# A four-layer trunk on one core: keys squared ahead of the tanh, another bank for the bonus product, two value buffers, transposes in pieces, and two copies that change engines

## The chip, the cores and the metric

The kernel runs on one core of a Trainium2 chip. The time is that of one execution on the device, in microseconds (us). Of the kernel before, three runs gave 1247.04, 1248.28 and 1244.97 us, median 1247.04. The traces name the engines PE (TensorE matmul), PEld (its weight loads), DVE (VectorE), ACT (ScalarE), POOL (GpSimd) and SP (SyncE). A name such as `L883` is a line of the kernel; the lines of the changed kernel stand up to two lower.

## The reference, cut to what matters

The trunk has 512 positions of 1024 channels in float32. Its layers are a gated spatial mixer, a gated feed-forward layer with a short convolution, an RWKV-7 time mixer, a second such feed-forward layer, and a last norm. All lines of the change lie in the time mixer:

```python
r = xr @ w_r;  k = xk @ w_k;  v = xv @ w_v
w = -softplus(-(w0 + tanh(xw @ w1) @ w2)) - 0.5      # decay
a = sigmoid(a0 + (xa @ a1) @ a2)
g = sigmoid(xg @ g1) @ g2                            # gate
kk = heads(k * k_k)
kk = kk * rsqrt(maximum(sum(kk * kk, -1), 1e-24))
k = k * (1 + (a - 1) * k_a)
y = wkv7_scan(r, exp(-exp(w)), k, v, -kk, kk * a)    # 16 heads of 64 channels
#   S_t = S_{t-1} diag(w_t) + (S_{t-1} a_t) b_t^T + v_t k_t^T ;  y_t = S_t r_t
y = (y - mean(y)) * rsqrt(var(y) + 64e-5) * ln_w + ln_b
bonus = sum(r_h * k_h * r_k, -1, keepdims=True) * v_h
out = ((y + bonus) * g) @ w_o
```

## The kernel before, in words

Activations lie transposed: 128 channels on the partitions, all 512 positions along the free axis, so that 1024 channels are eight tiles of 128x512. A dense product is made as three matmuls, high part by high part, high by low and low by high (`mm3`, L325, L326 and L327), which keeps float32 accuracy. The four layers run one after another. The accumulator memory (PSUM) is used through four tags, `mm`, `aux`, `e` and `us`, with two banks each; a tile that asks for a bank waits until the tile that held it has been read.

The time mixer replaces the step-by-step recurrence by chunks of 64 positions: within a chunk a triangular system is solved, and a state is handed from chunk to chunk. Its work comes in pieces, written as generators:

- `pairs` goes over the eight pairs of heads p = 0 to 7. For each, `decay` makes the decay factors (tanh, L906, running sum, exponentials) and the norm of the scaled keys (`kn` L908, its square `sq` L913, summed over the head by matmul L923, then L925 and L926). `operands` scales keys and receptances (L944 to L957). `products` makes the triangular blocks (matmul L973, masked on DVE at L977, copied by ACT at L978) and the factors of the state (L986 to L991).
- `projections` makes keys and values with dense matmuls. It is taken a step at a time as a filler between the other pieces. A value's accumulator is copied by ACT (L854) into the tile `v`, and `value` then transposes and centres it (L868, copies L873), multiplies the head sums of r·k (matmul L883) by `v` on DVE (L885) and adds the bias `ln_b` on ACT (L886). The result lies in `rt`, where the gate finds it.
- `invert(g)` inverts the triangular blocks of four pairs (g = 0 or 1). ACT (or DVE) copies the blocks into `ix` (L1046, L1048), DVE transposes them into `li` (L1051), solves 32x32 blocks by a long back-substitution (L1062 to L1070, small operations that depend on one another), and transposes the answer twice (L1051: into `ix` and into `li`). PE then builds the 64x64 inverses (L1090, L1093) with copies on ACT between (L1098, L1103).
- `scan(g)` handles eight chunks: PE L1301, copy `wt` on DVE (L1304), PE L1314 with the inverse, copies L1315 and L1316, PE L1321 and L1327, and so on. `finish` normalises the outputs, and `gate` (L1209) multiplies them by the gate before the output projection.

What order these take is settled when the program is built: the generators are woven, some with a note that they are issued behind a given PE instruction, and a scheduler writes one queue per engine. Each engine then takes its queue in that order. The scheduler's decisions change with every edit, so that an edit on one engine also moves rows on the others.

Of the kernel before, what the change touches and what calls it, by code (L numbers as in the profile page):

```python
# [12 lines left out]
F32 = mybir.dt.float32  # L13
F32R = mybir.dt.float32r
AF = mybir.ActivationFunctionType
ALU = mybir.AluOpType
# [4 lines left out]
P = 128  # L21
D = 1024
KT = 8
T = 512
# [120 lines left out]
class Emit:  # L145
# [622 lines left out]
    def rwkv_main(self, r, ctx, gain):  # L768
# [13 lines left out]
        def tmp(tag, bufs, w=W2):  # L782
            return tile_([P, w], tag, bufs)
# [12 lines left out]
        def second_factors(p):  # L796

            w32 = self.l2w.pop()
            l2[:] = [ep.tile([P, 2 * P], F32R, tag=f"l2{i}", bufs=1, name=self.uid("l2")) for i in range(3)]
            for j in range(2):  # L800
                w = w32[:, 512 * j:512 * j + 2 * P]
                S.copy(l2[j], w)
                V.tensor_tensor(l2[2][H[j]], w[H[j]], l2[j][H[j]].bitcast(F32), ALU.subtract)
            if p + 2 < KT:
                self.load_l2(p + 2)


        def projections():

            load = Ahead([lambda n=n, m=m: self.parts(n, m) for n in PARTS for m in range(KT)])  # L810

            def key(m, a):
                while m >= NKEY and m - NKEY not in used:
                    yield
                ks[m] = tmp("key", NKEY, T)
                S.copy(ks[m], a)

            for m in range(KT - 2):
                a = self.acc("mm")
                yield from self.dense_steps(a, load.take(), r.xk)  # L820
                yield from key(m, a)
                yield

            ws = [load.take(), load.take(False)]
            accs = [self.acc("mm") for _ in range(2)]
            xv = []
            for k in range(KT):
                for j in range(2):
                    self.mm3(accs[j], self.wcols(ws[j], k * P, P), r.xk[k], k == 0, k == KT - 1)
                while len(xv) < min(k + 3, KT):  # L830
                    xv.append(r.mix(3, len(xv)))
                if k == 4:
                    load.fetch()
                yield
            for j in range(2):
                yield from key(KT - 2 + j, accs[j])
            late = iter(())
            for m in range(KT):
                a = self.acc("mm")
                w = load.take()  # L840
                if m == KT - 2:
                    ga["w"] = load_gate(0)
                for n, _ in enumerate(self.dense_steps(a, w, xv)):
                    yield
                    next(late, None)
                    if m == KT - 1 and n == 0:
                        gw[0] = gate_weights(ga["w"])
                        ga["parts"] = self.gate_parts()
                    if m == KT - 1 and len(gx) < 2:
                        gx.append(gate_mix(len(gx)))  # L850
                for _ in late:
                    yield
                v = ip.tile([P, T], F32, tag="v", bufs=1, name=self.uid("v"))
                S.copy(v, a)  # L854
                late = value(m, v)
            next(late)
            tail.append(late)

        def value(m, v):
            g, i = divmod(m, 4)  # L860

            def bank():
                return self.acc("mm" if len(done) < KT else "aux")

            vt = ip.tile([P, NCH, C], F32, tag="vt", bufs=1, name=self.uid("vt"))
            q = bank()
            for b in range(4):
                nc.tensor.matmul(q[:, b * P:(b + 1) * P], v[:, b * P:(b + 1) * P], self.c("center", P),  # L868
                                 start=True, stop=True)
            q4 = q.rearrange("p (b h f) -> p b h f", b=4, h=2)  # L870
            for hd in range(2):
                for par in range(2):
                    S.copy(vt[H[1 - hd], par::2, :], q4[H[par], :, hd, :])  # L873
            nc.sync.dma_start(vtd[:, :, m].rearrange("c p f -> p c f"), vt)
            yield
            yield

            while m not in done:
                yield
            wb = ip.tile([P, P], F32, tag="wb", bufs=1, name=self.uid("wb"))  # L880
            S.activation(wb, self.c("bones", P), AF.Copy, scale=self.p("r_k", m))
            q = bank()
            nc.tensor.matmul(q, wb, rt[g][:, i, :], start=True, stop=True)  # L883
            b = rt[g][:, i, :]
            V.tensor_tensor(b, q, v, ALU.mult)  # L885
            S.activation(b, b, AF.Identity, bias=self.p("ln_b", m))  # L886
            vdone.add(m)
            yield


        def scratch(tag):
            return self.gp.tile([P, T], F32, tag=tag, bufs=2 if tag == "sq" else 1, name=self.uid(tag))

        def decay(p, u):
# [6 lines left out]
                nc.tensor.matmul(accs[j], l2[2][H[j], w], r.lr[j][H[j]], start=False, stop=True)  # L901
            if p % 2 == 1 and p + 1 < KT:
                second_factors(p + 1)
            th, u.ta = scratch("sq"), tmp("ta", 2, T)
            for j, x in enumerate((th, u.ta)):
                S.activation(x, accs[j], AF.Tanh, scale=0.5, bias=dq(j, p))  # L906
            u.kn = tmp("kn", 2, T)
            S.activation(u.kn, k, AF.Copy, scale=dq(2, p))  # L908
            V.tensor_scalar(th, th, 1.0, None, ALU.add)
            yield  # L910
            V.tensor_tensor_scan(th, self.c("smask", T), th, 0.0, ALU.mult, ALU.add)
            sq = scratch("sq")
            S.activation(sq, u.kn, AF.Square)  # L913
            u.gt = tile_([P, NCH, C + 1], "gt", 1)
            G.memset(u.gt[:, :, 0:1], 1.0)
            S.activation(u.gt[:, :, 1:], c3(th), AF.Exp, scale=C1)
# [110 lines left out]
        def invert(g):  # L1027
# [19 lines left out]
                if g == 1 and us.start == 0:  # L1047
                    yield  # L1048
            def turn(out, src):
                for bs in [slice(n, n + 8) for n in range(0, 32, 8)] if g == 1 else [slice(0, 32)]:  # L1050
                    V.transpose(out[:, bs], src[:, bs])  # L1051

            tt = blocks("li")
# [149 lines left out]
        def gate(g, i, ts, q=None):  # L1203

            if q is None:
                q = self.acc("aux")[:, 0:ts.stop - ts.start]
                opening(g, i, ts, q)
            o = rt[g][:, i, ts]
            V.tensor_tensor(o, o, q, ALU.mult)  # L1209
            while len(outs[g]) <= i:  # L1210
                outs[g].append(tuple(self.xr.tile([P, T], F32R, tag=t, bufs=10, name=self.uid(t)) for t in ("mxh", "mxl")))
            oh, ol = (x[:, ts] for x in outs[g][i])
            S.copy(oh, o)
            V.tensor_tensor(ol, o, oh.bitcast(F32), ALU.subtract)
# [52 lines left out]
        def scan(g, late=iter(())):  # L1267
# [15 lines left out]
            for c in range(NCH):  # L1283
# [17 lines left out]
                lead = batch(lambda i, hd, n: nc.tensor.matmul(us[H[hd], 0, i, :], both(i, hd, 0), vu[:, hd, i, :],  # L1301
                                                               start=True, stop=True))
                wt = tile_([P, 4, C], "wt", 4)
                V.tensor_copy(wt, us[:, 0])  # L1304
                batch(lambda i, hd, n: nc.tensor.matmul(e[H[hd], 0, i, :], st[i][H[hd], 0:C], vu[H[hd], hd, i, :],
                                                        start=i == 0, stop=False, skip_group_check=True), lead)
                if not last:
# [217 lines left out]
```

## Time and profile before

| what | us |
|---|---|
| median of three runs | 1247.04 (1244.97 to 1248.28) |
| the profiled execution | 1245.55 |
| its span, first to last instruction | 1243.7 |
| PE busy in the span | 1226.8 (99%) |
| DVE busy | 851.1 (68%) |
| ACT busy | 633.1 (51%) |
| POOL busy | 81.4 (7%) |
| mean granted TensorE clock | 0.996 |

The profile is of one execution; durations are from it. A row of the timeline reads: start in us, duration in us, engine, line, operation, tile written <- tiles read, shape, count, and in brackets the idle time of the engine ahead of it and what ended it. A row of the waits reads: engine, tile and line that waited, engine, tile and line waited for, total us, times, the longest. A row of the windows reads: stretch, its length and busy us (with the number of instructions) of PE, PEld, DVE, ACT and POOL, then the granted clock, the share of the DMA engines' time and GB/s. Matmuls overlap, so that what one costs is read from the distance between two starts. The pairs run from about 572 to 716 us, the first scan from about 725 on, and the time mixer ends near 885.

### The profile page before, as it was taken

How to read it: one execution, taken by the hardware profiler on the slowest of the kernel's cores; microseconds unless marked ns; L12 is line 12 of the kernel's file. 1: busy time of each engine (PE TensorE's matmuls, PEld its weight loads, DVE VectorE, ACT ScalarE, POOL GpSimd, SP SyncE). 2: the span in 40 equal slices, each digit the busy share in tenths (PEclk: the TensorE clock that was granted, in tenths of full speed). 3: DMA queues.
4: the chain of work that ended last, by engine and by line, in shares of the span. 5: the costliest groups of instructions: out<-in, count | busy, mean ns of one | idle time of the engine just before them, and what ended most of it. 6: DMA issues, size and time to landing. Idle time of an engine off the chain costs nothing.

```text
span 1243.7 us, 19411 instructions
## 1 busy us (share of the span) xinstructions
PE 1226.8 (99%) x7535; PEld 1000.2 (80%) x7535; DVE 851.1 (68%) x1418; ACT 633.1 (51%) x1089; POOL 81.4 (7%) x106
## 2 busy tenths in 40 slices
PE   9999999999999999999999999999999999999997
PEld 6878888888888888877887777778888888888886
DVE  5566578888876454675899698776777777872323
ACT  6544455555554343466787667424544444543232
POOL 1100200000000001000000013222000000000000
PEclk9999999999999999999999899999999999999999
DMA  7232457887556776326888797654223223333332
GB/s 273 94 105 82 132 180 246 246 249 241 192 172 193 220 226 196 109 81 182 220 242 237 188 280 233 219 171 135 85 102 102 90 97 102 97 88 104 97 93 81
DMA packets 125133, 201.65 MB, mean 162 GB/s; under 512 B 39857, under 2 KB 63153, under 8 KB 125041
## 3 DMA queue, kind: packets, MB, share of 16 engines
q10 hardware_dynamic: 38976, 112.87, 29.5%
q1 hardware_dynamic: 86064, 87.54, 22.6%
q8 instruction: 59, 0.97, 0.3%
q14 instruction: 34, 0.27, 0.1%
HBM read 152.93 MB, written 47.45 MB: 161 GB/s over the span
## 4 chain that ended last, share of the span: by engine, by line
PE 91%; DVE 4%; DMA 3%; ACT 1%; issue 0%; SPq 0%; POOL 0%; DVEq 0%; POOLq 0%; ACTq 0%
PE mm L325 9%; PE mm L327 9%; PE mm L326 9%; PE aux L325 6%; PE aux L326 6%; PE aux L327 6%; PE e L325 6%; PE e L326 6%; PE us L325 6%; PE e L327 6%; PE us L327 6%; PE us L326 6%; PE us L1314 1%; PE aux L973 1%; PE aux L988 1%; PE us L1321 1%
## 5 line engine op out<-in xcount | busy, mean ns | idle before, releaser
L237 ACT CAST w<-w 128x512 fp32r<-128x512 f32 x340 | 206.5, 611 | 359.8 <-PE aux L327 92.6
L238 DVE TENSOR_TENSOR w<-w,w 128x512 fp32r<-128x512 f32 x340 | 230.5, 680 | 180.2 <-ACT w L237 179.6
L325 PE MATMUL mm<-mxh,w 128*128 128x512 f32 x408 | 167.9, 412 | 2.7 <-DVE rt L885 2.6
L327 PE MATMUL mm<-mxh,w 128*128 128x512 f32 x408 | 161.1, 395 | 0.0
L326 PE MATMUL mm<-mxl,w 128*128 128x512 f32 x408 | 160.6, 394 | 0.0
L325 PEld LDWEIGHTS mm<-mxh,w 128*128 128x128 f32 x408 | 77.0, 189 | 22.8 <-DVE rt L885 3.3
L327 PEld LDWEIGHTS mm<-mxh,w 128*128 128x128 f32 x408 | 77.0, 189 | 17.1 <-issue 0.8
L326 PEld LDWEIGHTS mm<-mxl,w 128*128 128x128 f32 x408 | 77.1, 189 | 16.2 <-issue 1.7
L575 ACT ACTIVATE cv<-z,par 128x512 f32<-128x512 f32 x88 | 71.7, 817 | 26.5 <-DVE z L573 21.2
L325 PE MATMUL aux<-mxh,w 128*128 128x512 f32 x216 | 84.5, 391 | 0.0
L325 PE MATMUL us<-mxh,w 128*128 128x512 f32 x216 | 84.5, 391 | 0.0
L327 PE MATMUL aux<-mxh,w 128*128 128x512 f32 x216 | 84.2, 390 | 0.0
L326 PE MATMUL aux<-mxl,w 128*128 128x512 f32 x216 | 84.1, 389 | 0.0
L326 PE MATMUL us<-mxl,w 128*128 128x512 f32 x216 | 84.1, 389 | 0.0
L327 PE MATMUL us<-mxh,w 128*128 128x512 f32 x216 | 84.1, 389 | 0.0
L354 POOL TENSOR_TENSOR ss<-ss,sq 128x512 f32<-128x512 f32 x24 | 31.7, 1323 | 761.1 <-ACT sq L352 761.1
L325 PE MATMUL e<-mxh,w 128*128 128x512 f32 x208 | 81.4, 391 | 0.0
L326 PE MATMUL e<-mxl,w 128*128 128x512 f32 x208 | 81.1, 390 | 0.0
L327 PE MATMUL e<-mxh,w 128*128 128x512 f32 x208 | 81.0, 389 | 0.0
L576 DVE SCALAR_TENSOR_TENSOR cv<-z,par,cv 128x512 f32<-128x512 f32 x88 | 66.0, 752 | 19.5 <-ACT cv L575 19.5
L577 DVE SCALAR_TENSOR_TENSOR cv<-z,par,cv 128x512 f32<-128x512 f32 x88 | 66.0, 752 | 2.9
L325 PEld LDWEIGHTS aux<-mxh,w 128*128 128x128 f32 x216 | 40.5, 188 | 9.0 <-issue 0.5
(1113 smaller groups left out, 2555.2 us busy)
## 6 DMA issues: line engine op xcount, KB each, us to landing
w<-in_wup ACTq DMA_DIRECT2D x88, 512.0 KB, 3.7
w<-in_wdn ACTq DMA_DIRECT2D x32, 512.0 KB, 3.7
st<-std SPq DMA_DIRECT2D x15, 640.0 KB, 6.6
w<-wkd ACTq DMA_DIRECT2D x16, 512.0 KB, 5.1
w<-wvd ACTq DMA_DIRECT2D x16, 512.0 KB, 5.1
w<-wod ACTq DMA_DIRECT2D x16, 512.0 KB, 4.2
w<-in_wdn ACTq DMA_DIRECT2D x16, 384.0 KB, 3.3
w<-in_wsu ACTq DMA_DIRECT2D x8, 512.0 KB, 3.7
```

The source lines that it names most:

```text
L237: nc.scalar.copy(hi[r, :n], src)
L238: (lo_eng or nc.vector).tensor_tensor(lo[r, :n], src, hi[r, :n].bitcast(F32), ALU.subtract)
L325: mm(acc, wh, xh, start=first, stop=False)
L326: mm(acc, wh, xl, start=False, stop=False)
L327: mm(acc, wl, xh, start=False, stop=last)
L354: nc.gpsimd.tensor_tensor(self.ss, self.ss, self.sq, ALU.add)
L575: nc.scalar.activation(c, z[:, 2:], AF.Identity, scale=cw(2, i), bias=self.p("conv_b", l * 44 + i))
L576: nc.vector.scalar_tensor_tensor(c, z[:, 1:T + 1], cw(1, i), c, ALU.mult, ALU.add)
L577: nc.vector.scalar_tensor_tensor(c, z[:, 0:T], cw(0, i), c, ALU.mult, ALU.add)
L973: nc.tensor.matmul(qs[hd][:, c - ch.start, :], bk[H[hd], c, C * hd:C * hd + P], ar[H[hd], c, :], start=True, stop=True)
L988: nc.tensor.matmul(qs[hd][:, c, :], bk[H[hd], c, C * hd:C * hd + P], dg[H[hd], c, :], start=True, stop=True)
L1314: nc.tensor.matmul((us, ux)[hd][H[hd], 1, i, :], ti[g][H[hd], i, c, :], wt[H[hd], i, :], start=True, stop=True)
```

## The change

It has six parts, all in the time mixer.

1. The value tile `v` gets two buffers.
2. The bank of the bonus product L883 is `aux` when all pairs are done, `e` when the operands of the last pair have been issued, and otherwise `mm`; before, it was `mm` until all pairs were done.
3. The bias `ln_b` is no longer added by ACT in `value`, but inside the gate, whose DVE multiplication becomes a scalar_tensor_tensor (add, then multiply).
4. In `decay`, the scaled key and its square are issued ahead of the two tanh.
5. The transposes of the first inversion are made in four pieces of eight blocks each, as those of the second were.
6. The copy of `wt` in the scan moves from DVE to ACT.

```diff
-                v = ip.tile([P, T], F32, tag="v", bufs=1, name=self.uid("v"))
+                v = ip.tile([P, T], F32, tag="v", bufs=2, name=self.uid("v"))
...
-            q = bank()
+            q = self.acc("aux" if len(done) == KT else "e" if KT - 1 in used else "mm")
             nc.tensor.matmul(q, wb, rt[g][:, i, :], start=True, stop=True)
             b = rt[g][:, i, :]
             V.tensor_tensor(b, q, v, ALU.mult)
-            S.activation(b, b, AF.Identity, bias=self.p("ln_b", m))
...
+            u.kn, sq = tmp("kn", 2, T), scratch("sq")
+            S.activation(u.kn, k, AF.Copy, scale=dq(2, p))
+            S.activation(sq, u.kn, AF.Square)
             th, u.ta = scratch("sq"), tmp("ta", 2, T)
             for j, x in enumerate((th, u.ta)):
                 S.activation(x, accs[j], AF.Tanh, scale=0.5, bias=dq(j, p))
-            u.kn = tmp("kn", 2, T)
-            S.activation(u.kn, k, AF.Copy, scale=dq(2, p))
             V.tensor_scalar(th, th, 1.0, None, ALU.add)
             yield
             V.tensor_tensor_scan(th, self.c("smask", T), th, 0.0, ALU.mult, ALU.add)
-            sq = scratch("sq")
-            S.activation(sq, u.kn, AF.Square)
...
-                for bs in [slice(n, n + 8) for n in range(0, 32, 8)] if g == 1 else [slice(0, 32)]:
+                for bs in [slice(n, n + 8) for n in range(0, 32, 8)]:
                     V.transpose(out[:, bs], src[:, bs])
...
-            V.tensor_tensor(o, o, q, ALU.mult)
+            V.scalar_tensor_tensor(o, o, self.p("ln_b", 4 * g + i), q, ALU.add, ALU.mult)
...
-                V.tensor_copy(wt, us[:, 0])
+                S.copy(wt, us[:, 0])
```

**DVE, where the first inversion begins.** `lq` is the masked block of a pair (pair 5 under the first number, pair 6 under the later one), `sq` its decay argument, `n_963` the norm of pair 6, `li` the transposed blocks. Before:

```order
L977 TENSOR_TENSOR lq_5794<-aux_5784,cst 128x4x128
L977 TENSOR_TENSOR lq_5794<-us_5785,cst 128x4x128
L911 SCALAR_TENSOR_TENSOR sq_5775<-cst,sq_5775 128x512
L1051 STREAM_TRANSPOSE li_5820<-ix_5814 128x32x32
L1055 MEMSET li_5820 128x32
L1062 SCALAR_TENSOR_TENSOR li_5820<-li_5820 128x30
L1069 TENSOR_TENSOR pr_5815<-li_5820 128x58
L925 TENSOR_SCALAR n_963_5837<-e_5832 128x8
```

and in the changed kernel:

```order
L975 TENSOR_TENSOR lq_5796<-us_5787,cst 128x4x128
L909 TENSOR_SCALAR sq_5779<-sq_5779 128x512
L911 SCALAR_TENSOR_TENSOR sq_5779<-cst,sq_5779 128x512
L923 TENSOR_SCALAR n_963_5840<-e_5835 128x8
L924 RECIPROCAL n_963_5840<-n_963_5840 128x8
L975 TENSOR_TENSOR lq_5853<-aux_5843,cst 128x4x128
L1049 STREAM_TRANSPOSE li_5822<-ix_5816 128x8x32 x4
L975 TENSOR_TENSOR lq_5853<-us_5844,cst 128x4x128
L1053 MEMSET li_5822 128x32
```

The norm of pair 6 and the first half of its next mask moved from behind the transposes to in front of them, and the transpose became four. Further down the same queue three of the four pieces of the last transpose (`li_6289<-li_5822`) stand between operations of the back-substitution, where before one whole transpose stood at its end.

**ACT, the same place.** `ix` are the blocks to be inverted, `kn` the scaled key of pair 6 and the `sq` made from it its square, `ta` and the other `sq` the two tanh. Before:

```order
L906 ACTIVATE sq_5775<-e_5769,dpar 128x512
L906 ACTIVATE ta_5776<-e_5770,dpar 128x512
L908 ACTIVATE kn_5779<-key_5738,dpar 128x512
L1046 COPY ix_5814<-ti_4841 32x1024
L957 COPY bk_5761<-bk_5761 64x8x64
L1046 COPY ix_5814<-ti_4841 32x1024
L978 COPY ti_4842<-lq_5794 64x256
L1046 COPY ix_5814<-ti_4841 32x1024
L978 COPY ti_4842<-lq_5794 64x256
L1046 COPY ix_5814<-ti_4841 32x1024
L913 ACTIVATE sq_5824<-kn_5779 128x512
```

and in the changed kernel:

```order
L955 COPY bk_5761<-bk_5761 64x8x64
L904 ACTIVATE kn_5775<-key_5738,dpar 128x512
L908 ACTIVATE ta_5780<-e_5770,dpar 128x512
L905 ACTIVATE sq_5776<-kn_5775 128x512
L908 ACTIVATE sq_5779<-e_5769,dpar 128x512
L976 COPY ti_4842<-lq_5796 64x256 x2
L1044 COPY ix_5816<-ti_4841 32x1024 x2
```

The square moved from behind the last copy of `ix` to between the two tanh. Two of the four copies of `ix` stand a little further up, ahead of these rows.

**PE, where the first inversion's products begin.** `mm_6293` and `mm_6296` are the accumulator of value 4, `mm_6325` and `mm_6331` that of the transposes of value 3, and L1090 the first product of the inversion. Before:

```order
L327 MATMUL mm_6293<-mxh_5515,w_1020_6194 128x512
L868 MATMUL mm_6325<-cst,v_6291 128x128
L1090 MATMUL e_6306<-ix_6288,ti_4841 32x32 x16
L868 MATMUL mm_6325<-cst,v_6291 128x128 x3
L325 MATMUL mm_6293<-mxh_5522,w_1020_6194 128x512
L326 MATMUL mm_6293<-mxl_5523,w_1020_6194 128x512
```

and in the changed kernel:

```order
L327 MATMUL mm_6296<-mxh_5515,w_1020_6195 128x512
L868 MATMUL mm_6331<-cst,v_6294 128x128 x4
L325 MATMUL mm_6296<-mxh_5522,w_1020_6195 128x512
L1088 MATMUL e_6312<-ix_6288,ti_4841 32x32 x16
L326 MATMUL mm_6296<-mxl_5523,w_1020_6195 128x512
```

Three matmuls of L868 and one dense matmul moved in front of the inversion's first product (L1090 before, L1088 now). The bonus product of value 2 stands thirteen rows above in both orders, as `L883 MATMUL mm_6277<-rt_4333,wb_6275 128x512` before and `L883 MATMUL e_6278<-rt_4333,wb_6276 128x512` now. From pair 5 on, the products of the pairs stand some 15 dense matmuls earlier in PE's queue than before.

## The prediction

> **What bounds the kernel now.** I read the page's busy table first, then the waits of PE over the whole run, then PE, DVE and ACT row by row where these waits lie.
>
> ```profile
> PE 1226.8 (99%) x7535; PEld 1000.2 (80%) x7535; DVE 851.1 (68%) x1418; ACT 633.1 (51%) x1089; POOL 81.4 (7%) x106
> PE mm L325 <- DVE rt L885: 2.6, 2, 2.3
> PE us L1314 <- DVE wt L1304: 1.0, 2, 0.8
> PE e L923 <- ACT sq L913: 0.7, 1, 0.7
> PE e L899 <- DVE kn L950: 0.6, 1, 0.6
> PE e L1090 <- DVE ix L1051: 0.2, 1, 0.2
> ```
>
> PE is busy for 1226.8 of 1243.7 us (the span): the change adds one matmul to PE and removes none, so it can gain only PE's idle time and its time at a low clock. The five waits beneath (line waiting, line waited for, total, times, longest) touch edited lines and add up to 2.6 + 1.0 + 0.7 + 0.6 + 0.2 = 5.1 us, 0.4% of the run.
>
> The windows (PE, PEld, DVE, ACT and POOL busy, granted clock, DMA share, GB/s) say where:
>
> ```profile
> 625.00:650.00 25.00, 25.00 (x229) 20.77 (x225) 23.06 (x41) 20.21 (x39) 0.23 (x2) 1.00 0.80 229
> 675.00:700.00 25.00, 22.18 (x163) 16.96 (x163) 24.27 (x57) 12.73 (x27) 0.61 (x2) 0.96 0.94 258
> 695.00:700.00 5.00, 2.83 (x18) 2.13 (x20) 4.76 (x11) 2.33 (x4) 0.00 (x0) 0.80 0.81 222
> 700.00:705.00 5.00, 5.00 (x44) 4.31 (x40) 1.48 (x1) 3.41 (x6) 0.00 (x0) 0.52 0.09 33
> 760.00:765.00 5.00, 4.72 (x127) 3.65 (x124) 4.94 (x9) 4.95 (x10) 2.76 (x3) 1.00 0.99 245
> ```
>
> Up to 650 us the pairs leave PE no gap. At 675 to 700 it idles 2.8 us, while DVE is busy 24.27 of 25: there the back-substitution of the first inversion bounds, and PE has only dense matmuls to fill with. Right behind the longest gap the granted clock falls to 0.80 and then 0.52.
>
> ```profile
> 696.99 0.50 PE L325 MATMUL mm<-mxh,w 128*128 128x512 f32 x1 [2.28 <-DVE rt L885]
> 697.32 0.40 PE L326 MATMUL mm<-mxl,w 128*128 128x512 f32 x1
> 697.56 0.39 PE L327 MATMUL mm<-mxh,w 128*128 128x512 f32 x1
> 698.47 0.63 PE L327 MATMUL mm<-mxh,w 128*128 128x512 f32 x1
> 698.90 0.63 PE L868 MATMUL mm<-cst,v 128*128 128x128 f32 x2
> 699.72 1.07 PE L1090 MATMUL e<-ix,ti 32*32 32x32 f32 x32 [0.19 <-DVE ix L1051]
> 700.71 1.65 PE L868 MATMUL mm<-cst,v 128*128 128x128 f32 x6
> 704.72 0.43 PE L325 MATMUL mm<-mxh,w 128*128 128x512 f32 x1
> ```
>
> A dense matmul starts every 0.24 us (697.32, 697.56) and, from about 698 until 704.72, every 0.43 (698.47, 698.90). So some 6.7 us ran at about half speed, at a cost of about 3.3 us: the dip costs more than the gap ahead of it.
>
> **The change, part by part.** *Banks and values.* The 2.28 us at 696.99 is a dense accumulation that wants the `mm` bank in which L883 left its product; it is free only once DVE has reached L885, which stands deep in its back-substitution. With L883 of values 2 and 3 in `e`, this wait goes, and the 0.35 that makes 2.6 with it: 2.6 us removed.
>
> *Squares and products.* Moving kn and its square ahead of the tanh removes 0.7 at L923; the wait at L899 (0.6) goes since the products stand 15 or more dense matmuls earlier in PE's order. With 0.2 at L1090, 4.1 us of waits on edited lines disappear up to the first L1090.
>
> *Where they go.* Next late is `ix`. L1090 needs it transposed, and `ix` ends a chain on DVE alone:
>
> ```profile
> 656.56 2.02 DVE L1051 STREAM_TRANSPOSE li<-ix 128x1024 f32<-128x1024 f32 x1 [2.77 <-ACT ix L1046]
> 659.04 0.16 DVE L925 TENSOR_SCALAR n<-e 128x8 f32<-128x8 f32 x1
> 659.29 0.20 DVE L926 RECIPROCAL n<-n 128x8 f32<-128x8 f32 x1
> 660.79 0.68 DVE L977 TENSOR_TENSOR lq<-aux,cst 128x512 f32<-128x512 f32 x1
> 661.39 0.68 DVE L977 TENSOR_TENSOR lq<-us,cst 128x512 f32<-128x512 f32 x1
> 697.67 1.99 DVE L1051 STREAM_TRANSPOSE ix<-li 128x1024 f32<-128x1024 f32 x1
> 657.23 1.16 PE L923 MATMUL e<-cst,sq 128*128 128x128 f32 x8 [0.67 <-ACT sq L913]
> 715.96 2.24 DVE L1051 STREAM_TRANSPOSE li<-ix 128x256 f32<-128x256 f32 x4
> 759.27 0.60 DVE L1051 STREAM_TRANSPOSE ix<-li 128x256 f32<-128x256 f32 x1
> 759.74 0.62 DVE L1051 STREAM_TRANSPOSE li<-li 128x256 f32<-128x256 f32 x1
> ```
>
> That chain runs from 656.56 to 699.66 with DVE nearly full, so `ix` moves only by what is added to or taken from it:
>
> - Start. In the new order the norm (L925, L926) and the first mask (L977) of pair 6 stand ahead of the first transposes. PE reaches the matmuls for that mask at about (657.23 − 0.67) − 15 × 0.24 = 653.0; L923 with the first half of L973 takes 1.9 and the mask 0.6 (660.79 to 661.39), so the transposes start at about 655.5 to 656.0 instead of 656.56. I take −0.75.
> - These three operations no longer stand behind the transposes: 0.25 for the norm pair (about 0.12 each, start to start) and 0.60 for the mask, −0.85.
> - Three of the four pieces of the last transpose (`li`<-`li`) now stand inside the back-substitution, at 0.5 each (759.27 to 759.74): +1.5.
> - Four pieces cost 2.24 for one of 2.02: +0.2, at two places with 0.15 to 0.2 each: +0.35.
>
> Together −0.75 − 0.85 + 1.5 + 0.35 = +0.25: `ix` is ready at about 699.9, no earlier than before. PE gets there sooner and waits. On the way it also wants the four L868 of value 3, which stand whole ahead of L1090 now (one did before). They need ACT's copy of the value (L854):
>
> ```profile
> 695.01 0.40 ACT L881 ACTIVATE wb<-cst,par 128x128 f32<-128x128 f32 x1
> 696.97 0.73 ACT L886 ACTIVATE rt<-rt,par 128x512 f32<-128x512 f32 x1 [1.55 <-DVE rt L885]
> 697.60 0.56 ACT L854 COPY v<-mm 128x512 f32<-128x512 f32 x1
> ```
>
> Without L886 and with a second buffer the copy no longer waits for DVE's L885 and ends near 695.01 + 0.40 + 0.56 = 696.0. PE reaches the first of these L868 at 698.90 − 3.9 (the removed waits without L1090's) − 0.4 (two matmuls at full speed instead of half) = 694.6, so about 1.4 us come back there; four L868 and one dense matmul bring it to about 697.1, and it idles some 2.8 at L1090. What PE has done by then is three L868 and one dense matmul more, work that stood behind L1090: 1.65 at half clock for three L868 (700.71), about 0.8 at the full one, and 0.24, together 1.04, less the 0.25 by which `ix` slips: **0.8 us gained**. Bounds: 0 if `ix` slips by 1 us, and 4.1 if it comes as much earlier.
>
> *The clock.* 2.28 us of idle time led to 6.7 us near half clock. I expect about 4 us idle within 5.4 us, so I let the dip return: 0; bounds −3.3 if it vanishes, +3.3 if it lasts twice as long. [...]
>
> *Copies of wt on ACT, bias in the gate.* In the scan, L1314 waits for wt:
>
> ```profile
> L1304 DVE COPY wt<-us x16: 417/425/427, 727.8 to 835.6; 128x256 f32<-128x256 f32 x16
> 728.28 0.68 PE L1314 MATMUL us<-wt,ti 64*64 64x64 f32 x16 [0.78 <-DVE wt L1304]
> 729.04 0.37 ACT L1316 COPY rb<-us 64x256 f32<-64x256 f32 x1 [1.44 <-PE us L1314]
> 763.66 2.10 ACT L1098 COPY ti<-li 32x1024 f32<-32x1024 f32 x2
> L886 ACT ACTIVATE rt<-rt,par x8: 711/724/727, 671.1 to 761.2; 128x512 f32<-128x512 f32 x8
> L1209 DVE TENSOR_TENSOR rt<-rt,aux x8: 420/554/687, 796.5 to 826.6; 128x512 f32<-128x512 f32 x4, 128x256 f32<-128x256 f32 x4
> L576 DVE SCALAR_TENSOR_TENSOR cv<-z,par,cv 128x512 f32<-128x512 f32 x88 | 66.0, 752 | 19.5 <-ACT cv L575 19.5
> ```
>
> No ACT copy of 128x256 stands in the trace; it is priced between L1316 (64x256, 0.37) and L854 (128x512, 0.56), so about 0.4, like DVE's 0.425. The 1.0 us of waits on wt go where ACT is idle. Where it isn't (4.95 of 5 us from 760 on), I add three chunks that arrive one copy late, 3 × 0.4 = 1.2, less one L886 (0.72) that ACT is spared there: +0.5. Bounds: 0 if ACT always has room; +5.6 in the rival below. L886 itself (8 × 0.724 = 5.8 us of ACT) ends no wait of PE but those counted. L1209 becomes a scalar_tensor_tensor: at most 752 − 687 = 65 ns more on each 128x512, after 796, where DVE has room, hidden by PE's projections; uncovered it would be at most 16 × 65 ns, 1.0 us.
>
> **Sum**: −0.8 (inversion) + 0 (clock) − 1.0 + 0.5 (scan) = −1.3 us from the profiled execution's 1245.55 (span 1243.7, 1.85 around it), 1244.25. That execution lies 1.5 below the median of the three runs, 1247.04, by which the forecast is **1245.7**. A measurement can tell about 0.3% (3.7 us) from no change: this is inside.
>
> **Rivals.**
> *The dip goes (faster).* If the idle time at L868 and L1090 is broken into pieces that no longer lower the clock, 3.3 us come back: 1245.7 − 3.3 = 1242.4. For it: the longest piece may stay near 2.3, and the shares of the two are my guess. Against: the idle sum is larger than the gap that now does it. Chance 0.23. [...] With `ix` 1 us earlier as well it would be 1241.4; 0.03 for that and other gains.
> *ACT becomes the bound of the first scan (slower).* The wt copy queues on ACT behind the copies of the inversion (2.10 for two L1098 at 763.66) and of the values; eight chunks of scan 0 each come about 0.7 late, 8 × 0.7 = 5.6, against −1.3 − 0.5 already counted: 1247.04 − 1.8 + 5.6 = 1250.8. It decides once ACT's queue at L1314 is on average longer than one copy of 128x512. For it: ACT's 4.95 of 5 at 760 to 765. Against: 13.41 of 25 at 725 to 750, and POOL and DVE steps in each chunk that could cover it. Chance 0.12.
>
> ```profile
> 725.00:750.00 25.00, 24.21 (x340) 18.05 (x340) 24.00 (x59) 13.41 (x29) 5.94 (x8) 1.00 0.95 296
> ```
>
> *A second dip (slower).* L868 idles first and L1090 again; the clock halves for both, +3.3, and `ix` slips 1 us: 1245.7 + 4.3 = 1250.0. Chance 0.05.
>
> **How the numbers follow.** Forecast 0.57; the dip goes 0.23, other gains 0.03; ACT 0.12; second dip 0.05. Faster by over 0.3% needs less than 1243.3: 0.26. Slower needs more than 1250.8; I give both slow cases, at its edge, to it: 0.17. Within: 0.57. The range of 1240.5 to 1250.5 holds the forecast and the faster case and cuts half of the slow ones; the likeliest case by itself reaches from 1243.5 to 1247.5.
>
> **What will show it.** Right: no wait of L325 on L885 before the first inversion, no wait of L923 on the square; a wait of 2 to 3 us at the first product of the inversion (L1090's successor) for `ix`, with ix ready at 699 to 701; 1 to 2 us at the four L868 ahead of it; the clock near 0.5 for 5 us behind; the span of the scans unchanged within 1 us. Wrong: `ix` at 697 or earlier, a clock of 1.0 throughout, or waits on the ACT copy of wt of more than 2 us in sum.

## The result

The changed kernel is slower. Its median is 1251.14 us (eight runs, 1249.82 to 1253.95); the kernel before had 1244.90 in the runs beside it. The ratio is 1.0051, with a 95% interval of 1.0042 to 1.0060: about 6.2 us. Forecast were 1245.7 us and no difference that can be measured; the result also lies above the range, which ended at 1250.5. One run of E9 below, at 1517.5 us with a mean clock of 0.752, is left out of its median and ratio.

### The profile page after: what moved, and what is told of

Same layout as the page of the kernel before. It is cut to its first block, busy times and chain, and to the rows that moved or that the text cites. A ratio compares the mean times of both kernels' runs of the same rounds, so it can differ in the third digit from the quotient of the medians.

```text
span 1250.9 us, 19414 instructions
## 1 busy us (share of the span) xinstructions
PE 1228.8 (98%) x7535; PEld 1001.1 (80%) x7535; DVE 846.4 (68%) x1411; ACT 631.7 (50%) x1097; POOL 83.4 (7%) x106
## 5 line engine op out<-in xcount | busy, mean ns | idle before, releaser
L325 PE MATMUL aux<-mxh,w 128*128 128x512 f32 x216 | 84.5, 391 | 0.0
L325 PE MATMUL us<-mxh,w 128*128 128x512 f32 x216 | 84.5, 391 | 0.0
L238 DVE TENSOR_TENSOR pwl<-pw,pwh 128x512 fp32r<-128x512 f32 (+1 forms) x51 | 34.8, 683 | 19.2 <-DMA wod<-pwl 5.8
```

What stands on the lines that cost most here:

```text
L238: (lo_eng or nc.vector).tensor_tensor(lo[r, :n], src, hi[r, :n].bitcast(F32), ALU.subtract)
L325: mm(acc, wh, xh, start=first, stop=False)
```

## The profile after

The profiled execution took 1252.93 us (span 1250.9, where before had 1243.7). The page's busy table of the changed kernel:

```profile
PE 1228.8 (98%) x7535; PEld 1001.1 (80%) x7535; DVE 846.4 (68%) x1411; ACT 631.7 (50%) x1097; POOL 83.4 (7%) x106
```

and PE's largest waits in the time mixer (line that waits, line waited for, total us, times, longest; the line numbers are one or two lower than before from L886 on, so L898 is the old L899, L1088 the old L1090, L1319 the old L1321):

```profile
PE e L1088 <- DVE ix L1049: 2.9, 1, 2.9
PE e L898 <- DVE kn L948: 1.8, 1, 1.8
PE e L1324 <- issue: 1.1, 1, 1.1
PE us L1299 <- issue: 1.0, 2, 0.8
PE mm L325 <- DVE rt L885: 1.0, 1, 1.0
PE us L1319 <- DVE rb L1313: 1.0, 1, 1.0
PE mm L325 <- ACT mxh L1211: 1.0, 1, 1.0
PE us L1319 <- DVE vu L1313: 0.7, 1, 0.7
```

The waits for wt and for the square are gone and the long wait for L885 is gone, as forecast; one of 1.0 for value 1 is left, whose product still stands in `mm`. The wait for `ix` has become 2.9. But there is a row that the forecast had struck out, the one for kn (0.6 before, 1.85 now), and rows from the scan and its end. Of these only that of L1299 was there before, with 0.8, as L1301.

The windows (PE, PEld, DVE, ACT, POOL busy, granted clock, DMA share, GB/s) show where the clock is low:

```profile
645.00:650.00 5.00, 3.15 (x24) 1.94 (x20) 4.97 (x9) 4.90 (x8) 0.11 (x1) 0.96 0.79 188
650.00:655.00 5.00, 5.00 (x27) 3.76 (x27) 2.20 (x4) 4.04 (x7) 0.00 (x0) 0.70 1.01 299
700.00:705.00 5.00, 2.01 (x33) 1.70 (x34) 4.58 (x13) 0.90 (x3) 0.00 (x0) 0.92 0.86 231
705.00:710.00 5.00, 5.00 (x29) 3.78 (x23) 0.00 (x0) 4.42 (x7) 0.00 (x0) 0.50 0.33 76
735.00:740.00 5.00, 3.49 (x68) 2.86 (x69) 4.80 (x12) 1.73 (x4) 1.34 (x3) 1.00 1.05 302
```

The low clock behind the first inversion's wait has stayed; a second one stands at 649.6 to 653, behind the wait for kn. Before, PE had no idle time and no low clock from 640 to 656.

To see where the time went I divided each profiled execution at five events: A, the first matmul of pair 0's decay (L899 before); T, the first transpose (L1051); I, the first product of the inversion (L1090); B and C, the first and the last product with the inverse in the scans (L1314); and the end of the span. "Idle" and "clock" are PE's idle time and the time lost to the low clock (1 minus the granted clock), summed over windows of 1 us from 560 to 880. The ratio is that of the timed runs, with its interval; it is taken over all runs and can differ by 0.1% from the ratio of the medians. The rest is from one execution each. E1 to E18 are the experiments below.

| kernel | ratio | A-T | T-I | I-B | B-C | C-end | idle | clock |
|---|---|---|---|---|---|---|---|---|
| before | | 84.5 | 43.1 | 28.6 | 109.1 | 406.3 | 6.8 | 3.4 |
| changed | 1.0051 (1.0042-1.0060) | 88.2 | 43.9 | 27.9 | 111.7 | 406.9 | 11.6 | 5.1 |
| E1 squares back | 1.0036 (1.0024-1.0048) | 85.8 | 44.4 | 26.6 | 113.0 | 407.0 | 11.9 | 3.4 |
| E2 squares alone | 1.0054 (1.0039-1.0070) | 88.3 | 42.4 | 28.9 | 114.4 | 406.1 | 10.3 | 8.5 |
| E3 kn product first | 1.0030 (1.0019-1.0041) | 85.7 | 43.4 | 25.2 | 112.1 | 407.0 | 11.1 | 0.0 |
| E4 wt back on DVE | 1.0052 (1.0039-1.0065) | 88.3 | 43.8 | 27.7 | 108.8 | 407.3 | 10.0 | 3.4 |
| E5 wt on ACT alone | 1.0002 (0.9993-1.0011) | 86.0 | 43.6 | 25.7 | 110.2 | 406.3 | 8.5 | 1.7 |
| E6 pieces alone | 1.0000 (0.9991-1.0009) | 84.3 | 44.6 | 25.9 | 109.2 | 406.3 | 6.7 | 1.7 |
| E7 bias in gate alone | 1.0043 (1.0030-1.0056) | 84.3 | 43.1 | 27.1 | 114.2 | 406.9 | 10.2 | 5.1 |
| E8 banks, values alone | 1.0024 (1.0015-1.0033) | 84.3 | 43.0 | 29.8 | 109.5 | 406.3 | 7.8 | 3.4 |
| E9 bias back | 1.0043 (1.0028-1.0058) | 88.3 | 44.0 | 29.4 | 109.4 | 406.2 | 9.7 | 5.1 |
| E10 gap filled, nine | 1.0071 (1.0056-1.0085) | 86.8 | 47.2 | 25.6 | 116.1 | 407.0 | 9.7 | 3.4 |
| E11 dg on POOL | 1.0077 (1.0061-1.0093) | 85.2 | 45.8 | 28.0 | 114.6 | 406.6 | 13.0 | 5.1 |
| E12 E3 and bias back | 1.0025 (1.0015-1.0034) | 85.8 | 43.4 | 27.9 | 109.8 | 406.3 | 7.8 | 3.4 |
| E13 banks, values back | 1.0045 (1.0032-1.0058) | 86.9 | 44.7 | 25.4 | 115.4 | 406.9 | 12.1 | 5.1 |
| E14 gap filled, five | 1.0071 (1.0059-1.0083) | 86.8 | 43.9 | 29.4 | 111.0 | 407.0 | 9.5 | 1.7 |
| E15 squares, bias back | 1.0038 (1.0025-1.0051) | 84.3 | 44.6 | 28.2 | 110.7 | 406.3 | 8.8 | 3.4 |
| E16 squares, kn first | 1.0044 (1.0032-1.0056) | 85.8 | 42.2 | 26.7 | 114.3 | 406.2 | 10.0 | 3.4 |
| E17 bonus early | 1.0026 (1.0016-1.0036) | 84.3 | 43.2 | 27.2 | 111.9 | 406.3 | 8.4 | 1.7 |
| E18 bonus early, pieces | 1.0024 (1.0015-1.0033) | 84.3 | 44.6 | 27.2 | 109.8 | 406.3 | 7.6 | 1.7 |

Of the 7.2 us between the spans, 3.7 lie between A and T, 2.6 between B and C, 0.6 behind C. In PE's account they are 4.8 us of idle time and 1.7 of clock, with 0.7 in neither. That single executions differ by one or two low stretches has to be kept in mind in every row. They differ elsewhere too: A lies at 572.1 to 573.3 us, but at 575.5, 575.9 and 577.0 in E7, E16 and E3, which near 20 us wait 2.2 to 2.9 us for a weight; and A-T of E1 and E5 holds a wait of 1.3 and 1.5 us for the transfer of a weight. E3's profiled execution is the slowest of its eight runs for that reason: from A to the end it takes 673.4 us, the changed kernel 678.6.

How the 3.7 came about, in PE's and DVE's timeline of the changed kernel:

```profile
644.64 1.09 PE L929 MATMUL e<-cst,n 128*64 128x128 f32 x16
649.39 0.65 PE L898 MATMUL e<-lr,l 128*128 128x512 f32 x1 [1.85 <-DVE kn L948]
657.73 1.05 PE L921 MATMUL e<-cst,sq 128*128 128x128 f32 x8
646.03 0.69 DVE L964 TENSOR_TENSOR dg<-cst,gc 128x512 f32<-128x512 f32 x1
646.74 0.75 DVE L691 SCALAR_TENSOR_TENSOR mt<-h,omu,mt 128x512 f32<-128x512 f32 x1
647.44 0.69 DVE L949 SCALAR_TENSOR_TENSOR ta<-ta,rb 128x512 f32<-128x512 f32 x1
648.05 0.68 DVE L951 TENSOR_TENSOR ss<-ss,key 128x512 f32<-128x512 f32 x1
648.65 0.68 DVE L948 TENSOR_TENSOR kn<-kn,e 128x512 f32<-128x512 f32 x1
654.54 0.69 DVE L975 TENSOR_TENSOR lq<-aux,cst 128x512 f32<-128x512 f32 x1 [2.80 <-PE aux L971]
660.51 2.19 DVE L1049 STREAM_TRANSPOSE li<-ix 128x256 f32<-128x256 f32 x4
```

and the same place before:

```profile
647.97 0.70 PE L899 MATMUL e<-lr,l 128*128 128x512 f32 x2
647.43 0.68 DVE L950 TENSOR_TENSOR kn<-kn,e 128x512 f32<-128x512 f32 x1
648.03 0.69 DVE L951 SCALAR_TENSOR_TENSOR ta<-ta,rb 128x512 f32<-128x512 f32 x1
```

L929 writes the norm of pair 5 into an `e` bank, and L948 (L950 before) frees that bank. L929 is done at about 645.7; DVE is full (4.97 of 5 us from 645 to 650), and by the new order takes L691, L949 and L951 ahead of L948. Before, L950 stood ahead of the other products and was done when PE came for the bank. PE wants the bank at 647.5 for pair 6's decay and stands 1.85 us; the low clock that follows (3.4 us at 0.50, 1.7 us lost) makes it later still; DVE then idles 2.80 us for pair 5's products, and the transposes start at 660.51 instead of 656.56.

## The experiments

**The squares undone, alone, and with the late product mended.** E1 puts kn and its square back behind the tanh, E2 makes part 4 alone on the kernel before. E3 keeps the whole change and alters, in the program, only the order in which DVE's operations are issued:

```diff
+            bk = u.bk = tile_([P, NCH, 3 * C], "bk", 2)
             V.tensor_tensor(ar[:, :, 0:C], c3(kn), gt[:, :, 0:C], ALU.mult)
-            V.tensor_tensor(ar[:, :, C:], c3(rr), gt[:, :, 1:], ALU.mult)
+            V.tensor_tensor(kn, kn, u.q, ALU.mult)
+            with tc.issue_after(self.last(mybir.EngineType.DVE)):
+                V.tensor_tensor(ar[:, :, C:], c3(rr), gt[:, :, 1:], ALU.mult)
+                V.scalar_tensor_tensor(ta, ta, 1.0, ei, ALU.add, ALU.mult)
+                V.tensor_tensor(kp, kp, k, ALU.mult)
...
-            bk = u.bk = tile_([P, NCH, 3 * C], "bk", 2)
-            V.tensor_tensor(kn, kn, u.q, ALU.mult)
-            V.scalar_tensor_tensor(ta, ta, 1.0, ei, ALU.add, ALU.mult)
...
-            V.tensor_tensor(kp, kp, k, ALU.mult)
```

> The changed kernel with its fourth part undone (kn scaled and squared where it was before, behind the tanh); the other five parts stay. Theory A (the moved square makes the scheduler place pair 5's products earlier on PE and DVE's product of kn with the norm, which frees the e bank, behind three other operations; PE waits 1.85 us for it at pair 6's first matmul, the clock halves behind it, and the first inversion starts 4 us late): the wait of 1.85 is below 0.6, no low clock between 645 and 660, the first product of the inversion starts at 699 to 701 instead of 704.4, time 1245.5 to 1247.5. Theory B (the transposes in pieces, three of them inside the back-substitution, and the copies of wt on ACT make it slower): time stays at 1250 to 1252.

> The kernel before with the fourth part alone (kn scaled and squared ahead of the two tanh). Theory A: a wait of 1.5 to 2.2 us of pair 6's first matmul for kn times the norm, low clock behind it, inversion 3 to 5 us later than the 699.7 of before, time 1248 to 1250. Theory B: no difference that can be measured, 1244 to 1246.

> The changed kernel with one order of issue changed in the operands: kn times the norm stands right behind the first use of kn, and the receptance product, the ta product and the k product are issued behind it on DVE. All parts of the change stay, and PE's queue as well. Theory A: the wait of 1.85 us at pair 6's first matmul is below 0.4, no low clock between 645 and 660, transposes at 656 to 658 instead of 660.5, the first product of the inversion at 700 to 702; time 1247 to 1248.5 (1251.1 less 1.85 of wait and 1.5 of clock). Theory B: the wait was filled anyway, since the inversion ends with DVE: 1250 to 1252.

E1 gave 1249.13 us (ratio 1.0036): two of the six us, not the four to five that theory A put down. E2 gave 1253.5 (1.0054), with 1.9 us at pair 6's first matmul and 3.4 us of low clock behind it, and more time than A had allowed. E3 gave 1249.36 (1.0030), a little above theory A's range. From its timeline and windows (L944 is the product of kn there):

```profile
651.38 0.68 DVE L944 TENSOR_TENSOR kn<-kn,e 128x512 f32<-128x512 f32 x1
651.89 0.39 PE L898 MATMUL e<-lr,l 128*128 128x512 f32 x1
653.36 0.50 PE L325 MATMUL mm<-mxh,w 128*128 128x512 f32 x1 [1.08 <-ACT key L816]
654.85 0.39 PE L898 MATMUL e<-lr,l 128*128 128x512 f32 x1
655.00:660.00 5.00, 5.00 (x38) 4.17 (x37) 4.35 (x7) 4.56 (x8) 0.00 (x0) 1.00 1.08 307
```

The wait for kn is gone and no low clock follows; the transposes start 85.7 us after A, not 88.2. Against what was expected, PE's queue did move with the edit: six dense matmuls now stand between the two L898, and PE waits 1.08 us there for the copy of a key. So the late product is shown as a cause of the longer stretch A-T. In E1 that stretch, less the wait for the weight, is that of before. For the time, E3's interval just does not touch that of the changed kernel, and E1's overlaps a little.

**wt back on DVE, and each other part alone.** E4 is the changed kernel with `V.tensor_copy(wt, us[:, 0])`; E5, E6, E7 and E8 are the kernel before with part 6, 5, 3, and 1 with 2.

> The changed kernel with its sixth part undone (the copy of wt on DVE as before). Theory A (the copies only move which of two waits in the scan is the longer one: L1313 on DVE is the one that is late): the waits for wt come back (0.8 to 1.0 us), those for DVE's L1313 (1.7 us) fall by as much, time 1250.5 to 1251.5. Theory B (the copies cost the 2.5 us that the scan has become longer by): 1248 to 1249.

> The kernel before with the sixth part alone (copy of wt on ACT). Theory A (three profiles with this part took 111.7 to 113.0 us from the first to the last use of wt, before and the one without it 109.1 and 108.8: the copies make the scan about 3 us longer, as DVE's L1313 is late instead): first to last use of wt 111 to 113 us, new idle time of about 1 us each at the waits for L1313 and for the step after it, time 1247 to 1249. Theory B (that difference was the order of the other parts): 1244.5 to 1246.

> The kernel before with the fifth part alone (first inversion's transposes in four pieces). Theory A (three pieces inside the back-substitution lengthen the way to ix by 1.0 to 1.5 us, and PE waits for it): first transpose to first product of the inversion 44 to 45 us instead of 43.1, time 1245.5 to 1247.5. Theory B (PE has the three pieces' copies to do later and gains them back): 1244 to 1246.

> The kernel before with the third part alone (bias added in the gate). Theory A (the longer DVE operation delays the cast of the gated output: the wait of about 1 us near 855 that every kernel with this part shows and the one before does not): time 1245.5 to 1247, with that wait. Theory B (the 5.8 us that ACT is spared gain more): 1243 to 1245.

> The kernel before with the first and second part alone (two value buffers, bonus product in other banks). Theory A (the wait of 2.28 us for DVE's L885 goes, and comes back as a wait of 1.5 to 3 us for ix at the first product of the inversion): no gain but that of the work done ahead, 1244 to 1246, low clock for 0 to 6.8 us. Theory B (the wait is removed and the dip with it): 1240 to 1243.

E4 (1250.91) and E5 (1245.41 beside 1245.61) differ by nothing from what they are compared with; for E4 that is theory A, and in its trace a wait of 1.5 us for wt stands in place of those for L1313. Their B-C stretches (108.8 without the copies on ACT against 111.7; 110.2 against 109.1) are differences of single executions; theory A of E5 falls. E6 (1244.88) is the same as before too: its T-I is 1.5 us longer, as theory A had it, and I-B 2.7 shorter, most of which, 1.7 us, is less low clock in this execution.

E7 surprises: the bias in the gate alone costs 0.43% (1251.05), and E8 0.24% (1247.50); both lie above the ranges of their two theories. E8's waits are of the kind that the prediction had for the whole change:

```profile
PE mm L868 <- ACT v L854: 2.1, 1, 2.1
PE e L1093 <- ACT off L1103: 1.1, 1, 1.1
PE e L1090 <- DVE ix L1051: 0.9, 1, 0.9
PE mm L325 <- DVE rt L885: 0.3, 1, 0.3
```

The bank's wait of 2.3 is gone, and 3.0 us stand at L868 and L1090. Two stretches of low clock follow, of 3.4 us each, one behind these and one behind the wait for ACT's copy at L1093.

**The bias undone, and two parts undone.** E9 is the changed kernel with the bias back on ACT, E12 is E3 with that, E13 is the changed kernel with one value buffer and the old banks, E15 the changed kernel with parts 3 and 4 undone.

> The changed kernel with its third part undone (bias added by ACT in the value, gate a plain multiplication). Theory A (in the changed kernel the gate's longer DVE operation costs the wait of 0.95 us at the end of the scan and nothing else): that wait goes, a wait of L868 for the value's copy of 1.5 to 2.5 us as in the kernel with banks and values alone comes, time 1249 to 1251. Theory B (the part costs in company what it costs alone, 5 us): 1245 to 1247.

> The changed kernel with the earlier product of kn and with its third part undone. Theory A (each of the two gives what it gives by itself, 1.8 us and 0 to 2): 1247 to 1249.5, no wait at pair 6's first matmul, none of 0.95 us at the end of the scan. Theory B (the bias costs 5): 1243 to 1245.

> The changed kernel with its first and second part undone (one value buffer, bonus product in the banks of before). Theory A (these two parts cost about 2 us by themselves and do so in company): the wait of 2.3 us for DVE's L885 is there again, that of 2.93 at the first product of the inversion below 0.6, the wait of 1.85 at pair 6's first matmul stays; time 1248.5 to 1250. Theory B (the wait only stands in another place, at the same price): 1250.5 to 1252.

> The changed kernel with its third and fourth part undone; two value buffers, the other banks, the pieces and wt on ACT stay. Theory A (pieces and wt cost nothing, banks and values their 2 us, squares and bias make the rest): 1246.5 to 1248.5, with waits for the value's copy (2 us) and for ix (about 1 us). Theory B (banks and values need the other parts against them): 1249 to 1251.

Results: E9 1251.63 (1.0043) and E12 1249.03 (1.0025) beside 1245.37, E13 1248.85 (1.0045) and E15 1249.28 (1.0038) beside 1243.97. E12 and E13 came out as their theory A had it. E9 lies above both ranges, though its waits are those of theory A: none for L1211, and 2.1 for the value's copy. E15 lies in theory B's range, with theory A's wait for the value's copy (2.4) and none for `ix`. No part undone here brings the time back by itself, and neither do parts 3 and 4 together; part 5 was not undone. The parts alone (1 and 2 as one) cost 0.54, 0.43, 0.24, 0 and 0%, all six together 0.51%: they do not add up. One thing does repeat: C-end is 406.9 to 407.3 in every kernel with the bias in the gate and 406.1 to 406.6 in every one without. This 0.6 us, with the wait for L1211 in the profile, is the price of the longer gate operation at the end of the scan: on each 128x128 it took 280 ns before (L1209) and 344 in the changed kernel (L1207), eight times behind C, 0.5 us in all.

**The same wait taken away by other means.** E16 is E2 with E3's order; E17 is the kernel before with the two empty steps ahead of the bonus product taken out, E18 is that with the pieces.

```diff
             nc.sync.dma_start(vtd[:, :, m].rearrange("c p f -> p c f"), vt)
-            yield
-            yield
 
             while m not in done:
```

> The kernel before with the fourth part (squares ahead of the tanh) and with the earlier product of kn, nothing else; the fourth part alone took 1253.5. Theory A (its price is the late product and what comes of it: a later inversion, which meets the scan's copies on ACT at a bad place): no wait at pair 6's first matmul, none of 2.5 us in the scan for ACT's copy; 1244 to 1247. Theory B (the price is in the scan and stays): the 2.5 us and the low clock at 765 stay, 1249 to 1251.

> The kernel before with the bonus product of each value issued two steps of the filler earlier, so that DVE's L885 of value 2 stands fifteen operations further up in its back-substitution and the bank is free before PE wants it: the same wait taken away as by the other banks, by another means, with no other part of the change. Theory A (PE's wait at this place is set by ix, which ends with DVE's chain; taking the bank's wait away moves it to the first product of the inversion): no wait of 2.28 us for L885, one of 2 to 3 us for ix instead, time 1243.5 to 1246.5. Theory B (the bank's wait was worth its 2.28 us and the low clock behind it): 1238.5 to 1242.

> The same with the fifth part (transposes in pieces), by which four L868 and one dense matmul stand ahead of the first product of the inversion and not one L868. Theory A: the wait for ix 1.5 to 2.5 us, time 1243 to 1246, the version nearest to a gain over the kernel before. Theory B: 1238 to 1242.

E16 gave 1249.18 (1.0044): the wait for kn is gone, but theory B was right on the rest. E17 and E18 gave 1247.56 and 1247.61 beside 1244.61 (1.0026, 1.0024). In both the wait for L885 is gone and one of 1.5 to 1.6 for `ix` is there, as A had it, though shorter than the 2 to 3 it gave for E17; yet they are slower, and above the ranges of theory A. In E16, E17 and E18, and in E2, E7 and E11 (below), one row is new. From PE's and ACT's timeline of E17 (L1319 there is the old L1321, L1314 the old L1316, L1096 the old L1098):

```profile
761.33 0.69 PE L1319 MATMUL us<-vu,cbt 128*64 128x64 f32 x16 [2.46 <-ACT vu L1314]
756.31 1.50 ACT L873 COPY vt<-aux 64x256 f32<-64x256 f32 x4 [1.10 <-PE aux L868]
758.61 1.04 ACT L1096 COPY ti<-li 32x1024 f32<-32x1024 f32 x1 [0.80 <-DVE li L1049]
759.56 0.72 ACT L884 ACTIVATE rt<-rt,par 128x512 f32<-128x512 f32 x1
760.18 0.70 ACT L1112 ACTIVATE sq<-h,par 128x512 f32<-128x512 f32 x1
760.91 0.37 ACT L1314 COPY vu<-us 64x256 f32<-64x256 f32 x1
```

The copy that the scan waits for stands on ACT behind a copy of the second inversion, which waits for DVE, and two activations. Before, ACT's copy at this place (757.57) stands ahead of L873 (758.61). This is the place of the prediction's second rival, though wt was not on ACT in any of these six; in the kernels with wt on ACT this wait is 0.9 us or less, and so it is in E4, E6 and E8, with wt on DVE. That this wait is what makes the six slower is not shown: E18 has it (2.5), and its B-C is only 0.7 us longer than before.

**Work in the gap.** E10 and E14 put matmuls of constants in front of the inversion's first product, E11 moves one operation of each pair from DVE to POOL (`G.tensor_tensor(dg, ...)` on the kernel before).

```diff
-                    ps = self.acc("aux" if g == 1 else "e").rearrange("p (u t) -> p u t", t=32)
+                    ps = self.acc("aux" if g == 1 else "e")
+                    if g == 0 and i == 0 and hf == 0:
+                        for _ in range(9):
+                            nc.tensor.matmul(ps, self.c("center", P), self.c("smask", T), start=True, stop=True)
+                    ps = ps.rearrange("p (u t) -> p u t", t=32)
```

In E14 the nine are five.

> The changed kernel with nine matmuls of constants (128x512, about 0.46 us each, 4.1 in all) in front of the first product of the inversion, written into its bank and overwritten by it: they add nothing to the result. By the new order the four L868 and one dense matmul (1.1 us) stand behind the product again. Theory A (the half clock comes from the idle time ahead of it): PE's idle time there is below 1 us, the clock stays 1.00 from 700 to 712 instead of two stretches of 3.4 us at 0.50, so 3.4 us are won and 1.1 lost: 1248 to 1250. Theory B (the clock falls by itself, for instance after a time of full load, or the work filled in counts as little as idling): the low clock stays, 1251.5 to 1253.

> The changed kernel with five matmuls of constants in front of the first product of the inversion instead of nine: nine took 7.89 us, 0.87 each, and ended 3.4 us after ix was ready at 703.0; five end at about 703. They add nothing to the result. Theory A (idle time brings the half clock, and work in its place keeps it away): PE idle below 0.7 us between 698 and 706, clock 1.00 there and up to 715, time 1248 to 1250 (3.4 us of clock won, 1.1 us of work that stands behind the product again). Theory B (the low clock after 704 was no matter of the idle time): low clock again, 1251.5 to 1253.

> The kernel before with one DVE operation of each pair (the diagonal factor, 128x512, 0.68 us) on POOL, which is idle there. Theory A (the way to the first inversion's product is DVE's time, 43 us nearly full, so 2 operations less on it bring the product 1 to 1.3 us earlier): first transpose to first product 41.5 to 42.3 us instead of 43.1, time 1243 to 1245. Theory B (POOL is later than DVE was, and products wait for it): 1245.5 to 1249.

I had put a constant matmul at 0.46 us from the distance of L883 to its successor; it takes 0.87, so E10's nine ended 3.4 us after `ix` and its time (1254.51) says little. Its clock does:

```profile
700.00:705.00 5.00, 5.00 (x14) 2.13 (x13) 3.42 (x10) 1.36 (x2) 0.00 (x0) 1.00 0.63 179
705.00:710.00 5.00, 5.00 (x53) 3.62 (x52) 0.00 (x0) 4.95 (x6) 0.00 (x0) 1.00 0.00 0
```

and so it was in E14: with work in the gap the clock stayed at 1.00 up to 712. That agrees with the first half of theory A, but does not show it: in E3, E7, E16 and E17 the clock stayed at 1.00 there too, with gaps of 2.1, 2.2, 1.1 and 1.6 us and nothing in them. The other half does not hold: E14 took 1253.38. PE, now ahead, waited 1.8 us at 712 to 714 for an ACT copy of the inversion, with a low stretch of 3.4 us behind that. From T to B it needed 73.3 us, the changed kernel 71.8: the work set back behind the product and the new wait took more than the clock gave.

E11 gave 1255.25, the slowest of all. Its T-I is 45.8 us, not 41.5 to 42.3. DVE's chain itself became a little shorter: `ix` was done 42.5 us after T (699.93), before 43.1. But L885 of value 2 now stands behind that transpose, at 699.77 (before 696.25, ahead of it). PE waited 4.1 us for its bank, and so the first product came only at 703.25. Three operations of the back-substitution ran while POOL made the diagonal factor `dg`, and took 0.66, 0.52 and 1.05 us; others of the same shapes in this trace took 0.30, 0.40 and 0.30. No version here beats the kernel before; E5 and E6 equal it.

## Why the prediction was wrong, by its own steps

- *"The wait at L899 (0.6) goes since the products stand 15 or more dense matmuls earlier."* This step failed, and most of the stretch A-T with it. The products did move: the square's matmul of pair 5 stands at 637.77 instead of 641.64. The wait of 0.6, that of pair 7's decay for pair 6's kn, did go. But the forecast put nothing for the same operation one pair earlier, which DVE's new order set behind three others: 1.85 us came there, with 1.7 lost to the clock. E3 takes this wait and its low clock away; E1, without the moved square, does too.
- *Start of the transposes.* Forecast 655.5 to 656.0, measured 660.51: the term of −0.75 was +4.0, since PE reached the square's matmul of pair 6 at 657.73, not 653. The lower bound of the inversion's gain allowed for 1 us of slip of `ix`; its product came 4.7 us later.
- *The chain to `ix`.* The rest of this term was good: from T to I 44.1 us were worked out, 43.9 measured, and in E6 44.6 against 43.1 for the pieces.
- *Where the waits go.* Right in kind: the bank's wait reappears for `ix`, 2.93 us where 2.8 were forecast. That the size agrees is partly luck, since both `ix` and PE came more than 4 us later than forecast. The 1.4 at L868 did not come: the value's copy ended at 700.00 and not at 696.0, as ACT's queue stood 3.64 us for a mask on DVE, but PE also came only at 700.05. In E8, where L886 stays, that wait did come (2.1). The 0.35 us that the forecast struck out with the 2.28 belong to value 1, whose product stays in `mm`; they became 1.02. E17 and E18, where the bank's wait is taken away otherwise, also have a wait for `ix` in its place.
- *The clock.* The dip behind `ix` returned at the same length of 6.8 us, as forecast; the further 3.4 us, at 649.6, belong to the first point.
- *Scan.* The 1.0 of waits for wt went. Forecast −0.5 in sum, measured +2.6 in the profile: 1.7 for DVE's L1313 and 1.1 at L1324 are new. But E4 and E5 give no difference for the copies in the timed runs, so it isn't shown that these copies are the cause; what makes B-C longer is open.
- *The gate.* Forecast was that it is hidden, or uncovered at most 1.0: it is uncovered behind the scan, at 855.83, by 0.6.
- *Matmuls.* The forecast has PE with one matmul more; both profiles count 7535, and no line of the change issues one more.
- *Rivals.* By its time the nearest was ACT as the bound of the first scan, with 1250.8, but no wait for the copy of wt on ACT stands among PE's waits, so the nearness is luck. The second dip, with 1250.0, did come, but at another place than the one named there. A time mixer without any low clock was seen only in E3. That idle time in shorter pieces spares the clock, as the first rival supposed, was not shown: in E8 a low stretch of 3.4 us stands behind a piece of 1.1 us.

Term by term, in the two profiled executions: the inversion with its clock was put at −0.8 and came out at +3.8 (A to B), the scan at −0.5 and +2.6, the gate at 0 and +0.6. PE's waits in the time mixer grew by 4.6 us. Up to the first product of the inversion that is 1.3 for kn and 2.7 for `ix`, less 1.6 for the bank and 0.7 for the square; the scan adds 1.9 and the gate 0.95.

Shown is that three edits (squares; bias in the gate; banks and values) cost 0.24 to 0.54% alone, although each takes away a wait or work where it is made; in the profiles waits stand in other places, and the new order brought them. How the changed kernel's 6 us divide among the edits is not settled: undoing squares gives about 2, undoing any other part nothing that stands clear of the intervals, and with squares and bias undone 0.38% is left.

## What to carry to other kernels

Where a scheduler writes the queues, follow every operation that frees a bank through all its repetitions in the new order, and compare when its reader on the other engine arrives: the wait that a profile names may come back one round earlier (here 0.6 us went and 1.85 came). Where the chain that bounds runs on an engine that is full, a wait taken away ahead of its end can come back at its end (here 2.28 us for the bank, then 2.93 for `ix`). Give an edit that shifts the order a loss as likely as a gain, even where it removes work. Single profiles here lost between 0 and 8.5 us to low stretches of the clock (560 to 880 us); ratios of several runs decide.

## What the runs showed of the hardware

In the twenty profiled executions the low clock came, from 560 to 880 us, in stretches of 3.4 or 6.8 us at 0.50, so the loss there is in each a multiple of 1.7 us (0, 1.7, 3.4, 5.1 and 8.5 in the table). Gaps of PE of 1.0 to 2.5 us sometimes had one behind them and sometimes not: 1.02 us at 687 in the changed kernel and 2.2 us at 698 in E7 had none, the 1.1 us at L1093 in E8 had one. The same wait for kn of 1.85 to 1.9 us had one behind it in the changed kernel and in E2, E4 and E9, and none in E10, E13 and E14. E10's windows there read:

```profile
645.00:650.00 5.00, 3.13 (x26) 2.07 (x22) 4.97 (x10) 4.88 (x7) 0.12 (x1) 1.00 0.77 182
650.00:655.00 5.00, 4.94 (x31) 3.78 (x32) 3.54 (x8) 4.82 (x11) 0.00 (x0) 1.00 1.04 294
```

So the length of a gap did not decide by itself whether a low stretch followed; what did was not shown. In the eight runs of the changed kernel a lower mean clock goes, on the whole, with a longer time: 1249.82 us at 0.997, 1252.93 at 0.994, 1253.95 at 0.995. These runs of one kernel lie up to 4.1 us apart, so part of what separates two versions by a few us in single runs here is chance.
